# Broadcasting the decay rows in 2 KB pieces into the decay tiles, and alternating two PSUM banks, in a hybrid DeltaNet encoder layer

## The chip, the cores and the metric

The kernel runs on one core of one Trainium2 chip. The metric is device time in microseconds (us) for one execution, lower is better. Three executions were timed: 1382.4, 1386.79 and 1385.83 us, with a median of 1385.83 us.

## The reference, cut to what matters

One encoder layer over 512 positions of 1024 channels, batch 1, all in float32: a half-step SwiGLU FFN (width 2816), a token mixer, a second half-step FFN, a final RMSNorm. The mixer is where the change lies. One projection of the normed input gives, among others, q, k and v of 8 heads (128 channels each), which go through a short convolution of width 5 and SiLU. Each head then runs a gated delta rule over chunks, once left to right and once right to left:

```
qkv = silu(dwconv(dn_qkv, conv_dn));  q = l2norm(q) * DK**-0.5;  k = l2norm(k)
g = cumsum(-exp(a_log) * softplus(al + dt_bias))          # per chunk, per head, per direction
decay = exp(where(incl, g[..., :, None] - g[..., None, :], -inf))
a_mat = where(strict, (k*beta) @ k.T * decay, 0) + eye    # inverted by a triangular solve
attn  = (q @ k.T) * decay
state = state * exp(g_last) + (k * exp(g_last - g)).T @ v_new
```

So each head needs its cumulative decay g twice: as a column (one value per position, on partitions) and as a row broadcast over all 128 partitions, from which `decay` is made. It needs the products k·k and q·k within each chunk, the squares of k and q summed over channels, and k and v with positions on partitions.

## The kernel before, in words

Channels lie on partitions, 512 positions along the free dimension. Every weight product is done as three float32r matmuls (high part by high part, low by high, high by low; lines 186 to 188) over 128x128 weight tiles. `weight` loads 512 KB of raw weights into one of three `raw` buffers on SP's queue (L169), and ScalarE (ACT) and VectorE (DVE) split it into `hi` (L174) and `lo` (L176) in halves of 4 tiles, three buffers each. One raw load so feeds two hi/lo pairs, each pair 12 matmuls. These products fill TensorE (PE) through the whole program: first FFN, the mixer's 60 projections of 24 matmuls, the second FFN.

In the mixer the products are the filler between eight heads' DeltaNet work. `build(hd)` is a generator of ten steps: three short convolutions (each on one projection), SiLU of q, k and v and the decay broadcast, transposes of k, v and q to positions-on-partitions (`tok`), small per-head scales (`st`), the two decay tiles `ef` and `eb`, and twice (`c2`) a pair of chunks of key products. The table `EMIT` says in which sequence steps of `build` (b0 to b7), the triangular inversion (`invert`, for heads 0 to 2, 3 to 5, 6 and 7), `place`/`merge`, `scan` and the filler projections are recorded. The framework's scheduler then sets each engine's order from recorded order and priorities; weight loads and splits have a priority raised by 600. Within an engine, order is fixed: an instruction that waits holds all behind it, SP's queue of transfers too.

The decays: the cumulative decays `G` (128 positions by direction, chunk, head) are transposed on PE (L420), copied (L422) and written to DRAM as `grow` (L424). For each head, L469 reads its 8 rows of 128 values back into `Gb` (128 partitions by 8 by 128, 512 KB), every partition getting all 8 rows. `Gb` has one buffer, so a head's load waits for the last read of the head before. DVE reads it for `wj` and `el` in `st` (L514, L516) and for the subtraction into `ef` and `eb` (L528). ACT takes the exponentials of `st` (L517, L518), and Abs and Exp of `ef`, `eb` (L531 to L533).

The banks: PSUM has eight; three are `acc` for the products, two `ch` for the scan, and `o`, `kq`, `tp` one each. All transposes of `tok` go through `tp`: k, then v, then q. k's and q's transposes are also squared straight from the bank (L484), four ACT instructions each, so the bank stays taken until the last square:

```
                    if dst is not None:
                        act.copy(dst[:].rearrange("p c x -> p (c x)"), ps[:])
                    if sq is not None:
                        for c in range(NC):
                            act.activation(out=junk[:], in_=ps[:, c * P : c * P + P], func=ACT.Square,
                                           accum_out=ss[:, sq, c : c + 1])
```

Both pairs of chunks of key products (L547, L548) use the one bank `o`. It is read by `nl` (L552) and `at` (L556) on DVE, so the second pair's matmuls wait for the first pair's `at`. `kq` is used in the mixer by nothing else than a row-norm broadcast at its edges.

Of the kernel before, what the change touches and what calls it, by code (L numbers as in the profile page):

```python
# [7 lines left out]
F32 = mybir.dt.float32  # L8
F32R = mybir.dt.float32r
I32 = mybir.dt.int32  # L10
ACT = mybir.ActivationFunctionType
# [5 lines left out]
P = 128  # L17
# [5 lines left out]
NC = T // P  # L23
H = 8
# [29 lines left out]
def tile_layer(  # L54
# [23 lines left out]
    nc = tc.nc  # L78
    pe, act, dve, pool = nc.tensor, nc.scalar, nc.vector, nc.gpsimd

    def open_pool(stack, name, bufs=1, **kw):
        if "space" not in kw:
            kw["reuse_waits"] = "tile"
        return stack.enter_context(tc.tile_pool(name=name, bufs=bufs, **kw))
# [8 lines left out]
    psx = open_pool(ctx, "psx", bufs=1, space=PSUM)  # L93
    psum_ch = open_pool(ctx, "psum_ch", bufs=CH, space=PSUM)

    def bank(tag="acc", pool_=None):
        return (pool_ or psum).tile([P, 512], F32, tag=tag, name=tag, **({"bufs": TP} if tag == "tp" else {}))
# [14 lines left out]
    h = open_pool(first, "big", side="right").tile([P, KT, T], F32, tag="big", name="h")  # L112
# [12 lines left out]
    for k in range(KT):  # L125
# [3 lines left out]
        sq = sp0.tile([P, T], F32, tag="sq0", bufs=4, name="sq0")  # L129
# [6 lines left out]
    for i in range(2):  # L136
        ps = bank("o", psx) if i else bank("ch", psum_ch)
# [181 lines left out]
    def mixer(st, u, h, post):  # L319
# [3 lines left out]
        scr = open_pool(st, "scr", bufs=2, space=DRAM)  # L323
# [20 lines left out]
        wk = open_pool(dn, "wk", bufs=2)  # L344
        one = open_pool(dn, "one", bufs=1)
        with ExitStack() as dd:
            beta = dnc.tile([P, NC, 16], F32, name="beta")
            G = dnc.tile([P, 2, NC, H], F32, name="G")
# [15 lines left out]
            ps = bank("ch", psum_ch)  # L364
# [16 lines left out]
            ps = bank("tp", psx)  # L381
# [4 lines left out]
            x = dt.tile([P, NC, 16], F32, tag="spx", name="spx")  # L386
# [21 lines left out]
            for d in range(2):  # L408
                dve.scalar_tensor_tensor(
                    out=g[:, d], in0=x[:, :, d * H : d * H + H], scalar=-1.0,  # L410
                    in1=nea[:, d * H : d * H + H].unsqueeze(1).to_broadcast([P, NC, H]),
                    op0=ALU.mult, op1=ALU.mult)
            ps = bank("tp", psx)
# [5 lines left out]
            ps = bank("tp", psx)  # L419
            pe.transpose(ps[0:64, 0:P], G[:].rearrange("p d c h -> p (d c h)"), ident[:])  # L420
            gt = dt.tile([64, P], F32, tag="gt", name="gt")
            act.copy(gt[:], ps[0:64, 0:P])  # L422
            grow = scr.tile([2 * NC, H, P], F32, tag="grow", name="grow")
            nc.sync.dma_start(grow[:].rearrange("a h p -> (a h) p"), gt[:])  # L424
            early_half(T // 2, T)

        with dn:
# [20 lines left out]
            def short_conv(i):  # L448

                ps = project(12 + i)  # L450
                acc = cp.tile([P, T], F32, tag="cacc", name="cacc")
                taps(acc, ps, cvd_sb[:, i], 5)
                return acc

            def build(hd, s):
                cq = short_conv(hd)
                yield
                ck = short_conv(8 + hd)
                yield
                cv = short_conv(16 + hd)  # L460
                yield
# [3 lines left out]
                act.activation(out=kT[:], in_=ck[:], func=ACT.Silu)  # L465
                vT = cv
                act.activation(out=vT[:], in_=cv[:], func=ACT.Silu)
                Gb = wk.tile([P, 8, P], F32, tag="Gb", bufs=1, name="Gb")
                nc.sync.dma_start(Gb[:], grow[:, hd, :].unsqueeze(0).to_broadcast([P, 8, P]))  # L469

                yield

                ss = slot.tile([P, 2, NC], F32, tag="ss", name="ss")
                junk = one.tile([P, P], F32, tag="junk", name="junk")

                def tok(src, dst, sq):
                    ps = bank("tp", psx)
                    for c in range(NC):
                        pe.transpose(ps[:, c * P : c * P + P], src[:, c * P : c * P + P], ident[:])
                    if dst is not None:  # L480
                        act.copy(dst[:].rearrange("p c x -> p (c x)"), ps[:])
                    if sq is not None:
                        for c in range(NC):
                            act.activation(out=junk[:], in_=ps[:, c * P : c * P + P], func=ACT.Square,  # L484
                                           accum_out=ss[:, sq, c : c + 1])

                kt = s["kt"] = slot.tile([P, NC, P], F32, tag="kt", name="kt")
                tok(kT, kt, 0)
                vt = s["vt"] = slot.tile([P, NC, P], F32, tag="vt", name="vt")
                tok(vT, vt, None)  # L490
                tok(qT, None, 1)
                yield
                st_ = s["st"] = slot.tile([P, 8, 8], F32, tag="st", name="st")
# [8 lines left out]
                ns, sb, nr, wj, el = (st_[:, 2], st_[:, 3, 0:NC], st_[:, 4], st_[:, 5], st_[:, 6])  # L502
# [8 lines left out]
                dve.tensor_mul(brk, beta[:, :, hd], rk)  # L511
                for d in range(2):
                    last = (P - 1, 0)[d]
                    dve.tensor_sub(wj[:, d * NC : d * NC + NC], Gb[:, d * NC : d * NC + NC, last],  # L514
                                   G[:, d, :, hd])
                    dve.tensor_copy(el[:, d * NC : d * NC + NC], Gb[:, d * NC : d * NC + NC, last])  # L516
                act.activation(out=wj, in_=wj, func=ACT.Exp)  # L517
                act.activation(out=el, in_=el, func=ACT.Exp)  # L518

# [1 line left out]

                yield

                ef = wk.tile([P, NC, P], F32, tag="E", bufs=2, name="ef")
                eb = wk.tile([P, NC, P], F32, tag="E", bufs=2, name="eb")
                for d, m, op in ((0, ef, ALU.add), (1, eb, ALU.min)):
                    for c in range(NC):
                        dve.tensor_scalar(out=m[:, c, :], in0=Gb[:, d * NC + c, :],  # L528
                                          scalar1=G[:, d, c, hd : hd + 1], scalar2=0.0, op0=ALU.subtract,
                                          op1=op)  # L530
                act.activation(out=ef[:], in_=ef[:], func=ACT.Abs)  # L531
# [7 lines left out]
                nl = s["nl"] = slot.tile([P, 2, NC, P], F32, tag="nl", bufs=NL, name="nl")  # L539
                at = s["at"] = slot.tile([P, 2, NC, P], F32, tag="at", name="at")  # L540
                for c2 in range(2):
                    ps = bank("o", psx)
                    pk = ps[:].rearrange("p (c z x) -> p c z x", c=2, z=2)
                    for i in range(2):
                        c = 2 * c2 + i
                        sl = slice(c * P, c * P + P)
                        pe.matmul(pk[:, i, 0, :], kT[:, sl], kT[:, sl], start=True, stop=True)  # L547
                        pe.matmul(pk[:, i, 1, :], kT[:, sl], qT[:, sl], start=True, stop=True)  # L548
                    for i in range(2):
                        c = 2 * c2 + i  # L550
                        for d, m in ((0, ef), (1, eb)):
                            dve.scalar_tensor_tensor(out=nl[:, d, c, :], in0=pk[:, i, 0, :],  # L552
                                                     scalar=ns[:, d * NC + c : d * NC + c + 1],
                                                     in1=m[:, c, :], op0=ALU.mult, op1=ALU.mult)
                    for d, m in ((0, ef), (1, eb)):
                        dve.tensor_tensor(out=at[:, d, 2 * c2 : 2 * c2 + 2, :], in0=pk[:, :, 1, :],  # L556
                                          in1=m[:, 2 * c2 : 2 * c2 + 2, :], op=ALU.mult)
                    v = at[:, 0, 2 * c2 : 2 * c2 + 2, :]
                    pool.affine_select(out=v, in_=v, pattern=[[0, 2], [1, P]], compare_op=ALU.is_ge,
                                       fill=0.0, base=0, channel_multiplier=-1)  # L560
                    yield
# [398 lines left out]
    with ExitStack() as st:  # L960
        u, h, ssum = mixer(st, u2, h, ctx)
# [81 lines left out]
```

## Time and profile before

| what | value |
|---|---|
| median of three executions | 1385.83 us |
| the profiled execution: its own time, its span | 1384.16 us, 1382.1 us |
| PE busy / weight loads busy | 1339.7 us (97%) / 1112.8 us (81%) |
| DVE busy / ACT busy / POOL busy | 804.8 (58%) / 566.4 (41%) / 64.1 us (5%) |
| granted TensorE clock, mean over the span | 0.992 |
| DMA: moved, rate | 193.46 MB, mean 140 GB/s |
| mixer, from its first products to its merge | about 387 to 915 us of the span |

The page's first part gives each engine's busy time over the span. A busy PE of 97% says that PE is the engine to watch, and little of where the rest went: matmuls overlap in the records, so the start times in a timeline tell the pace. A window view gives the same figures for any stretch, with the granted clock and the DMA engines' busy share. The chain of waits runs back from the last instruction and names at each step what released it.

### The profile page before, as it was taken

The page shows a single profiled execution, that of the slowest core. Times are in us where ns is not written, and L with a number is a line of the kernel's source. Part 1 is how long each engine was busy: PE and PEld are TensorE (multiplying, and loading weights), DVE is VectorE, ACT ScalarE, POOL GpSimd, SP SyncE. Part 2 cuts the span into 40 slices and gives each one's busy share as a digit, 9 for nine tenths or more (in the row PEclk, how much of TensorE's full clock was granted, in tenths as well). Part 3 has the DMA queues.
Part 4 walks back from the last instruction along what each step waited for, and adds up shares of the span by engine and source line. Part 5 has one row for each costly group of instructions (what it writes and reads, how often), then busy time and mean ns, then how long its engine had stood idle before and what let it go on. Part 6 is the DMA issues. An engine that isn't in the chain of part 4 may idle for free.

```text
span 1382.1 us, 19594 instructions
## 1 busy us (share of the span) xinstructions
PE 1339.7 (97%) x7417; PEld 1112.8 (81%) x7417; DVE 804.8 (58%) x1745; ACT 566.4 (41%) x1150; POOL 64.1 (5%) x103
## 2 busy tenths in 40 slices
PE   6999999999998899999999999999999999999997
PEld 4888888888887778778777787888798888888886
DVE  6865555555375778786864785647553444443333
ACT  3333333322256664467555334545433333332330
POOL 0000000000000100021112001000000000000000
PEclk9999999999999999999999999999999999999999
DMA  8656566555434443333541433557503334333332
GB/s 319 218 159 191 181 193 191 171 172 182 130 126 94 124 130 127 121 116 107 130 139 60 124 113 95 168 197 245 176 31 104 125 109 134 124 108 95 100 100 71
DMA packets 86591, 193.46 MB, mean 140 GB/s; under 512 B 24737, under 2 KB 35169, under 8 KB 86370
## 3 DMA queue, kind: packets, MB, share of 16 engines
q1 hardware_dynamic: 71008, 164.29, 38.6%
q10 hardware_dynamic: 15490, 27.94, 5.9%
q8 instruction: 58, 0.95, 0.3%
q14 instruction: 35, 0.29, 0.1%
HBM read 171.19 MB, written 21.00 MB: 139 GB/s over the span
## 4 chain that ended last, share of the span: by engine, by line
PE 80%; DMA 8%; DVE 5%; issue 3%; ACT 3%; POOL 1%; ACTq 0%; POOLq 0%; SPq 0%; DVEq 0%
PE acc L188 22%; PE acc L186 22%; PE acc L187 22%; DMA msb<-gtd 2%; DMA Gb<-grow 2%; PE acc L918 1%; DVE lo L176 1%; PE ch L674 1%; PE ch L918 1%; PE o L697 1%; PE ch L685 1%; DMA raw<-w_in 1%; DVE cacc L444 1%; PE tp L610 1%; ACT hi L174 1%
## 5 line engine op out<-in xcount | busy, mean ns | idle before, releaser
L186 PE MATMUL acc<-uh,hi 128*128 128x512 f32 (+1 forms) x1224 | 473.3, 387 | 2.0 <-DVE sps L397 0.9
L187 PE MATMUL acc<-uh,lo 128*128 128x512 f32 (+1 forms) x1224 | 473.8, 387 | 0.7 <-DVE lo L176 0.7
L188 PE MATMUL acc<-ul,hi 128*128 128x512 f32 (+1 forms) x1224 | 472.3, 387 | 0.0
L174 ACT CAST hi<-raw 128x512 fp32r<-128x512 f32 (+1 forms) x416 | 252.2, 612 | 535.1 <-PE acc L188 479.0
L176 DVE TENSOR_TENSOR lo<-raw,hi 128x512 fp32r<-128x512 f32 (+1 forms) x416 | 280.4, 681 | 293.1 <-ACT hi L174 291.7
L186 PEld LDWEIGHTS acc<-uh,hi 128*128 128x128 f32 x1224 | 231.2, 189 | 44.4 <-ACT cacc L439 1.1
L187 PEld LDWEIGHTS acc<-uh,lo 128*128 128x128 f32 x1224 | 231.2, 189 | 42.3 <-DVE lo L176 1.3
L188 PEld LDWEIGHTS acc<-ul,hi 128*128 128x128 f32 x1224 | 230.8, 189 | 41.2
L186 PE MATMUL acc<-gh,hi 128*128 128x512 f32 (+1 forms) x396 | 144.9, 366 | 0.0
L187 PE MATMUL acc<-gh,lo 128*128 128x512 f32 (+1 forms) x396 | 144.6, 365 | 0.0
L188 PE MATMUL acc<-gl,hi 128*128 128x512 f32 (+1 forms) x396 | 144.4, 365 | 0.0
L150 DVE SCALAR_TENSOR_TENSOR raw<-raw,cs 128x1024 f32<-128x1024 f32 x72 | 87.9, 1223 | 59.8 <-DMA raw<-w_ada 59.7
L187 PEld LDWEIGHTS acc<-gh,lo 128*128 128x128 f32 x396 | 74.4, 188 | 12.1
L186 PEld LDWEIGHTS acc<-gh,hi 128*128 128x128 f32 x396 | 74.4, 188 | 12.1
L188 PEld LDWEIGHTS acc<-gl,hi 128*128 128x128 f32 x396 | 74.4, 188 | 12.1
L444 DVE SCALAR_TENSOR_TENSOR cacc<-acc,cvd_sb,cacc 128x510 f32<-128x510 f32 (+1 forms) x96 | 71.1, 742 | 4.3 <-ACT cacc L439 3.8
L313 DVE TENSOR_TENSOR sa<-sa,acc 128x512 f32<-128x512 f32 x40 | 27.4, 685 | 34.9 <-PE acc L188 33.2
L228 POOL TENSOR_TENSOR rs<-ms,mhalf 128x2 f32<-128x2 f32 (+1 forms) x7 | 6.2, 887 | 840.1 <-DVE ms L225 840.1
L196 ACT CAST gh<-sa 128x512 fp32r<-128x512 f32 x44 | 27.4, 622 | 18.4 <-DVE sa L313 13.7
L197 DVE TENSOR_TENSOR gl<-sa,gh 128x512 fp32r<-128x512 f32 x44 | 30.3, 692 | 5.5 <-PE tp L918 2.1
L206 ACT ACTIVATE sq<-h 128x512 f32<-128x512 f32 (+1 forms) x25 | 14.1, 563 | 47.3 <-DVE h L255 46.9
L584 DVE TENSOR_TENSOR A<-A,tmp 96x30 f32<-96x30 f32 (+29 forms) x90 | 29.0, 322 | 1.5
(270 smaller groups left out, 1454.4 us busy)
## 6 DMA issues: line engine op xcount, KB each, us to landing
raw<-w_ada SPq DMA_DIRECT2D x72, 512.0 KB
raw<-w_in SPq DMA_DIRECT2D x60, 512.0 KB
raw<-w2u SPq DMA_DIRECT2D x44, 512.0 KB
raw<-w1u SPq DMA_DIRECT2D x36, 512.0 KB
raw<-w1d SPq DMA_DIRECT2D x16, 512.0 KB
raw<-w2d SPq DMA_DIRECT2D x16, 512.0 KB
wf<-w1f SPq DMA_DIRECT2D x8, 512.0 KB
Gb<-grow SPq DMA_DIRECT2D x8, 512.0 KB
```

What stands on the lines that cost most here:

```text
L150: dve.scalar_tensor_tensor(out=raw[:], in0=raw[:], scalar=1.0, in1=cs[:], op0=ALU.mult, op1=ALU.mult, accum_out=part[:, n : n + 1])
L174: act.copy(hi[:], raw[:, k : k + n, :])
L176: dve.tensor_sub(lo[:], raw[:, k : k + n, :], hi[:].bitcast(F32))
L186: pe.matmul(ps[:, t0:t1], wh, rh[:, k0 + k, t0:t1], start=a, stop=False)
L187: pe.matmul(ps[:, t0:t1], wl, rh[:, k0 + k, t0:t1], start=False, stop=False)
L188: pe.matmul(ps[:, t0:t1], wh, rl[:, k0 + k, t0:t1], start=False, stop=b)
L196: act.copy(hi, src)
L197: dve.tensor_sub(lo, src, hi.bitcast(F32))
L313: dve.tensor_mul(sa[:], sa[:], ps[1][:])
L444: dve.scalar_tensor_tensor(out=acc[:, lo:hi], in0=src[:, lo + o : hi + o], scalar=w[:, i : i + 1], in1=acc[:, lo:hi], op0=ALU.mult, op1=AL ...
L584: dve.tensor_tensor(out=A[:, j + 1 : 32, 0:j], in0=A[:, j + 1 : 32, 0:j], in1=tv, op=ALU.add)
L918: pe.matmul(early[m][:], terms[i][0][:, m, :], terms[i][1], start=k == 0 and i == 0, stop=k == KT - 1 and i == 2)
```

## The change

`grow` becomes one row of 512 values per head and direction. Each head's broadcast is two transfers of 256 KB, straight into the tiles that become `ef` and `eb`, each partition getting 2 KB in one piece; they are recorded one to two steps earlier (after k's convolution) and those tiles have four buffers in place of two, `Gb` being gone. The subtraction works in place. v's transposes and the second pair of key products use bank `kq`. k's squares read the SBUF copy `kt`.

```diff
-            grow = scr.tile([2 * NC, H, P], F32, tag="grow", name="grow")
-            nc.sync.dma_start(grow[:].rearrange("a h p -> (a h) p"), gt[:])
+            grow = scr.tile([H, 2, NC * P], F32, tag="grow", name="grow")
+            nc.sync.dma_start(grow[:].rearrange("h d (c p) -> (d c) h p", p=P), gt[:])
...
                 ck = short_conv(8 + hd)
+
+                E = [wk.tile([P, NC, P], F32, tag="E", bufs=4, name=x) for x in ("ef", "eb")]
+                for d in range(2):
+                    nc.sync.dma_start(E[d][:].rearrange("p a b -> p (a b)"),
+                                      grow[hd, d : d + 1, :].to_broadcast([P, NC * P]))
...
-                Gb = wk.tile([P, 8, P], F32, tag="Gb", bufs=1, name="Gb")
-                nc.sync.dma_start(Gb[:], grow[:, hd, :].unsqueeze(0).to_broadcast([P, 8, P]))
...
-                def tok(src, dst, sq):
-                    ps = bank("tp", psx)
+                def tok(src, dst, sq, tag="tp"):
+                    ps = bank(tag, psx)
...
-                            act.activation(out=junk[:], in_=ps[:, c * P : c * P + P], func=ACT.Square,
-                                           accum_out=ss[:, sq, c : c + 1])
+                            act.activation(out=junk[:], in_=ps[:, c * P : c * P + P] if dst is None else dst[:, c, :],
+                                           func=ACT.Square, accum_out=ss[:, sq, c : c + 1])
...
-                tok(vT, vt, None)
+                tok(vT, vt, None, "kq")
...
-                    dve.tensor_sub(wj[:, d * NC : d * NC + NC], Gb[:, d * NC : d * NC + NC, last],
-                                   G[:, d, :, hd])
-                    dve.tensor_copy(el[:, d * NC : d * NC + NC], Gb[:, d * NC : d * NC + NC, last])
+                    dve.tensor_sub(wj[:, d * NC : d * NC + NC], E[d][:, :, last], G[:, d, :, hd])
+                    dve.tensor_copy(el[:, d * NC : d * NC + NC], E[d][:, :, last])
...
-                ef = wk.tile([P, NC, P], F32, tag="E", bufs=2, name="ef")
-                eb = wk.tile([P, NC, P], F32, tag="E", bufs=2, name="eb")
+                ef, eb = E
...
-                        dve.tensor_scalar(out=m[:, c, :], in0=Gb[:, d * NC + c, :],
+                        dve.tensor_scalar(out=m[:, c, :], in0=m[:, c, :],
...
-                    ps = bank("o", psx)
+                    ps = bank(("o", "kq")[c2], psx)
```

The scheduler gives a new order on every engine. Line numbers of the changed kernel differ by up to five (L469 becomes L462, L479 L481, L481 L483, L484 L486, L514 L516, L516 L517, L517 L518); L528 to L560 keep theirs. Three places follow.

**SP's queue of transfers, from the write of `grow` on** (L469 and L462 the broadcasts, L169 raw weights, L568 and L574 transfers of the inversion). Before, 9 rows:

```order
L424 DMA grow<-gt 64x128
L469 DMA Gb<-grow 128x8x128
L169 DMA raw<-w_in 128x1024
L469 DMA Gb<-grow 128x8x128
L169 DMA raw<-w_in 128x1024 x3
L568 DMA dl<-nl 128x1024
L574 DMA A<-dl 8x32x32
L169 DMA raw<-w_in 128x1024
L469 DMA Gb<-grow 128x8x128
```

Now:

```order
L424 DMA grow<-gt 8x8x128
L462 DMA ef<-grow 128x512
L462 DMA eb<-grow 128x512
L462 DMA ef<-grow 128x512
L462 DMA eb<-grow 128x512
L169 DMA raw<-w_in 128x1024 x3
L568 DMA dl<-nl 128x1024
L462 DMA ef<-grow 128x512
L169 DMA raw<-w_in 128x1024
L462 DMA eb<-grow 128x512
```

The broadcasts of heads 0 and 1 go out together right behind `grow`, and head 2's right behind head 0's `dl`, one raw load between its two halves.

**ACT, head 0's copies, squares and exponentials.** Before, 12 rows:

```order
L481 COPY kt<-tp 128x512
L484 ACTIVATE junk,ss<-tp 128x128
L517 ACT_TABLE_LOAD
L517 ACTIVATE st<-st 128x8
L484 ACTIVATE junk,ss<-tp 128x128
L518 ACTIVATE st<-st 128x8
L531 ACTIVATE ef<-ef 128x512
L174 CAST hi<-raw 128x512
L484 ACTIVATE junk,ss<-tp 128x128
L532 ACTIVATE ef<-ef 128x512
L484 ACTIVATE junk,ss<-tp 128x128
L533 ACTIVATE eb<-eb 128x512
```

Now:

```order
L483 COPY vt<-kq 128x512
L174 CAST hi<-raw 128x512
L483 COPY kt<-tp 128x512
L518 ACT_TABLE_LOAD
L518 ACTIVATE st<-st 128x8
L486 ACTIVATE junk,ss<-kt 128x128
L519 ACTIVATE st<-st 128x8
L531 ACTIVATE ef<-ef 128x512
L486 ACTIVATE junk,ss<-kt 128x128
L532 ACTIVATE ef<-ef 128x512
L486 ACTIVATE junk,ss<-kt 128x128
L533 ACTIVATE eb<-eb 128x512
```

The exponential of `st`, which needs the broadcast, still stands ahead of k's squares, but those squares no longer hold bank `tp`: the copy ahead of it does that alone. v's transposes now stand on PE ahead of the transposes that make `grow` (L420), in bank `kq`.

**DVE, where head 2's first read of the broadcast meets head 1's key products** (`nl` and `at` free the bank of the products). Before, 12 rows:

```order
L514 TENSOR_TENSOR st<-Gb,G 128x4
L516 COPY st<-Gb 128x4
L444 SCALAR_TENSOR_TENSOR cacc<-acc,cvd_sb,cacc 128x511
L514 TENSOR_TENSOR st<-Gb,G 128x4
L552 SCALAR_TENSOR_TENSOR nl<-o,st,ef 128x128
L444 SCALAR_TENSOR_TENSOR cacc<-acc,cvd_sb,cacc 128x510
L176 TENSOR_TENSOR lo<-raw,hi 128x512
L552 SCALAR_TENSOR_TENSOR nl<-o,st,eb 128x128
L552 SCALAR_TENSOR_TENSOR nl<-o,st,ef 128x128
L552 SCALAR_TENSOR_TENSOR nl<-o,st,eb 128x128
L556 TENSOR_TENSOR at<-o,ef 128x256
L556 TENSOR_TENSOR at<-o,eb 128x256
```

Now, 12 rows that begin with that read:

```order
L516 TENSOR_TENSOR st<-ef,G 128x4
L444 SCALAR_TENSOR_TENSOR cacc<-acc,cvd_sb,cacc 128x511
L176 TENSOR_TENSOR lo<-raw,hi 128x512
L444 SCALAR_TENSOR_TENSOR cacc<-acc,cvd_sb,cacc 128x511
L444 SCALAR_TENSOR_TENSOR cacc<-acc,cvd_sb,cacc 128x510 x2
L176 TENSOR_TENSOR lo<-raw,hi 128x512
L444 SCALAR_TENSOR_TENSOR cacc<-acc,cvd_sb,cacc 128x511
L552 SCALAR_TENSOR_TENSOR nl<-o,st,ef 128x128
L444 SCALAR_TENSOR_TENSOR cacc<-acc,cvd_sb,cacc 128x511
L552 SCALAR_TENSOR_TENSOR nl<-o,st,eb 128x128
L176 TENSOR_TENSOR lo<-raw,hi 128x512
L444 SCALAR_TENSOR_TENSOR cacc<-acc,cvd_sb,cacc 128x510
```

One read of head 2's broadcast still stands ahead of head 1's `nl` and `at`; its transfer stands much earlier in SP's queue, and the reads of its other half (L517, L516 of `eb`) now follow head 1's last `at`.

## Rows read from the trace of the kernel before

**Rows 1.** Windows: stretch, length, engines' busy (x instructions), granted clock, DMA share, GB/s.

```profile
430.00:510.00 80.00, 68.91 (x316) 56.12 (x315) 54.38 (x160) 50.80 (x120) 7.81 (x12) 0.91 0.45 115
...
442.00:448.00 6.00, 6.00 (x18) 4.80 (x18) 4.35 (x6) 4.25 (x7) 0.64 (x1) 0.55 0.43 89
...
448.00:470.00 22.00, 21.91 (x109) 18.14 (x108) 19.19 (x64) 17.05 (x46) 3.47 (x5) 1.00 0.43 135
```

**Rows 2.** Timeline of PE, first stall: start, us, instruction, [idle before <-releaser].

```profile
437.24 0.39 PE L186 MATMUL acc<-uh,hi 128*128 128x512 f32 x1
441.78 1.12 PE L479 MATMUL tp<-ident,cacc 128*128 128x128 f32 x4 [4.15 <-ACT junk L484]
...
447.66 0.40 PE L187 MATMUL acc<-uh,lo 128*128 128x512 f32 x1
...
448.56 0.39 PE L186 MATMUL acc<-uh,hi 128*128 128x512 f32 x1
448.79 0.40 PE L187 MATMUL acc<-uh,lo 128*128 128x512 f32 x1
```

**Rows 3.** Timeline of PE, one group of key products at full pace.

```profile
455.73 0.39 PE L547 MATMUL o<-kT 128*128 128x128 f32 x2
...
456.62 0.60 PE L479 MATMUL tp<-ident,qT 128*128 128x128 f32 x4
```

**Rows 4.** Timeline of PE, second and third stall.

```profile
474.55 0.39 PE L186 MATMUL acc<-uh,hi 128*128 128x512 f32 x1
478.36 0.77 PE L547 MATMUL o<-kT 128*128 128x128 f32 x2 [3.43 <-DVE at L556]
...
481.77 0.40 PE L188 MATMUL acc<-ul,hi 128*128 128x512 f32 x1
...
502.73 0.39 PE L188 MATMUL acc<-ul,hi 128*128 128x512 f32 x1
506.07 0.76 PE L547 MATMUL o<-kT 128*128 128x128 f32 x2 [2.96 <-DVE at L556]
...
509.06 0.40 PE L186 MATMUL acc<-uh,hi 128*128 128x512 f32 x1
```

**Rows 5.** The chain of waits: start, us, what; the broadcasts on it.

```profile
428.29 10.03 DMA Gb<-grow
...
464.64 9.63 DMA Gb<-grow
...
489.27 8.80 DMA Gb<-grow
```

**Rows 6.** Timelines of ACT and DVE: what the three broadcasts held up.

```profile
438.69 0.21 ACT L517 ACTIVATE st<-st 128x8 f32<-128x8 f32 x1 [4.10 <-DVE st L514]
...
474.29 0.17 DVE L514 TENSOR_TENSOR st<-Gb,G 128x4 f32<-128x4 f32 x1 [3.91 <-DMA Gb<-grow]
...
498.10 0.17 DVE L514 TENSOR_TENSOR st<-Gb,G 128x4 f32<-128x4 f32 x1 [3.62 <-DMA Gb<-grow]
```

**Rows 7.** A window during the first broadcast; ACT's queue in page part 3.

```profile
433.00:436.00 3.00, 3.00 (x15) 2.45 (x14) 0.00 (x0) 1.57 (x4) 0.00 (x0) 1.00 1.03 81
...
q10 hardware_dynamic: 15490, 27.94, 5.9%
```

**Rows 8.** Groups of convolution taps, `lo` splits, squares: count, busy us, mean ns, idle.

```profile
L176 DVE TENSOR_TENSOR lo<-raw,hi 128x512 fp32r<-128x512 f32 (+1 forms) x416 | 280.4, 681 | 293.1 <-ACT hi L174 291.7
...
L444 DVE SCALAR_TENSOR_TENSOR cacc<-acc,cvd_sb,cacc 128x510 f32<-128x510 f32 (+1 forms) x96 | 71.1, 742 | 4.3 <-ACT cacc L439 3.8
...
L484 ACT ACTIVATE junk<-tp 128x128 f32<-128x128 f32 x64 | 17.9, 280 | 5.4 <-PE tp L479 3.3 <-PE acc L187 1.0
...
L713 ACT ACTIVATE junk<-on 128x128 f32<-128x128 f32 x32 | 9.9, 308 | 6.8 <-DVE on L705 3.4 <-DVE rr L714 1.8 <-DVE A L584 1.1
```

**Rows 9.** Timelines of SP and ACT: a raw load held up, and its first cast.

```profile
616.63 1.20 SPq L169 DMA_DIRECT2D raw<-w_in  x2
...
632.29 0.62 ACT L174 CAST hi<-raw 128x512 fp32r<-128x512 f32 x1
```

## The prediction

> **What bounds the kernel now.** The busy times of the table above say that PE is busy for 97% of the span, so no other engine can set the end except by letting PE wait. The next question is where PE does not run at its pace, and the windows answer it: the stretch from 430 to 510 us has 68.91 us of PE in 80, at a mean granted clock of 0.91, where the mixer begins its heads [rows 1]. The reader should see that 11 us are missing there, and that what ran was partly at the lower clock. The timeline of PE through the mixer then shows three stops of over 1.5 us, all in this stretch. A product matmul at full pace starts 0.23 us after the last (448.56 to 448.79) [rows 2].
>
> First place: PE stands from 437.24, waiting 4.15 us for ACT's squares (L484) to leave bank `tp`; only at 447.66 is the pace back [rows 2]. After the stall the granted clock of 442 to 448 is 0.55, near the lower of the two levels (1.2 of 2.4 GHz) [rows 1]: PE had done nothing before. Between 437.24 and 447.66 lie 13 product matmuls and one group of four transposes. At pace these take 13 x 0.23 plus 0.44 (from 447.66 to 448.56 there are two products and one such group: 0.90 - 0.46), so 3.4 us. They took 10.4. **Loss: 7.0 us**, over half of it the wait, the rest the clock.
>
> Second and third: the second pair of key products waits for bank `o`, that is for DVE's `at`, 3.43 and 2.96 us [rows 4]. From 474.55 to 481.77 there are five product matmuls and a group of key products (0.89 us at pace [rows 3]), worth 5 x 0.23 + 0.89 = 2.0 us; they took 7.2: **loss 5.2 us**. From 502.73 to 509.06, four and a group, 1.8 us; they took 6.3: **loss 4.5 us** [rows 4].
>
> The three together are 16.7 us. What stands behind each is told by the chain of waits: the broadcast into `Gb` [rows 5]. It takes 10.03, 9.63 and 8.80 us to land, the second and third start only when DVE has read `Gb` for the head before, and what waits is: ACT, 4.10 us, for the scales (its squares of k stand behind them in order), and DVE, 3.91 and 3.62 us, with `nl` and `at` behind [rows 6].
>
> **The change, part by part.**
>
> *The broadcast in 2 KB pieces.* Bytes stay at 512 KB per head. While a broadcast ran, the 16 DMA engines were at 1.03 of their capacity and moved 81 GB/s [rows 7]: 243 KB cost 3.1 us of all sixteen, so a head's 524 KB some 6.7. ACT's queue, whose transfers here are nearly all 2 KB rows, put 27.94 MB through 5.9% of 1382.1 us [rows 7]: 2.9 us per MB, 1.5 us for a head. If the difference comes off the landing, 10.0 becomes about 4.9 us. The bounds: from below the 1.5 us of moving alone, from above no gain, 10.0. I take 5, since the saturated engines are the row nearest to the cause. The Trainium skill ("DMA: Bandwidth & Descriptors", Specifications) gives 512 B as the smallest transfer at line rate, and `Gb`'s pieces are 512 B, so by that rule the new pieces gain nothing and a head still takes 10 us. By that rule the engines should not be full at 81 GB/s, as the row has them.
>
> *Earlier, and four buffers.* Heads 0 and 1 get all four halves right behind `grow`, and head 2's wait no longer for head 1's subtraction but for head 0's `at`. In DVE's new order eight convolution taps and three `lo` splits stand, beside shorter work, between that `at` and the first read of head 2's half: 8 x 0.74 + 3 x 0.68 = 8.0 us [rows 8]. A landing of 5 us leaves 3 of slack. The waits of DVE on the second and third broadcast go; behind a 10 us landing some 2 us each would stay.
>
> *The banks.* k's squares no longer hold `tp`, and v's transposes stand in `kq`, before `grow` is even written. PE's next use of `tp` needs only the copy of k, which ACT makes ahead of the exponential. So the first stall loses both its causes, and a late broadcast no longer reaches PE at that point. The second pair of key products goes to `kq` and doesn't wait for `at` of the first pair. Each of the second and third stall loses both causes too.
>
> *What it adds.* (a) Eight more DMA issues on SP, under half a microsecond each; SP waits most of the time. (b) 32 squares read SBUF: 308 ns in place of 280 [rows 8], 0.9 us of ACT over the whole mixer, hidden behind PE's products; on the path it would be those 0.9. (c) New waits for banks: `tp` waits for k's copy where q's transposes follow closely; `kq` is shared by v's transposes and key products, and in four heads only a few product matmuls stand between the one and the other. From below nothing; from above a copy behind a cast, both as long as the cast's 0.62 us [rows 9], in each of seven heads: 8.7 us. I take 2, half a microsecond in four heads. (d) The subtraction in place and the strided reads keep their shapes: nothing. (e) Density: with the stalls gone, the 54.4 us of DVE and 50.8 of ACT in this stretch [rows 1] must fit into 63, 86% and 81%. The stretch from 448 to 470 ran with DVE at 87% and ACT at 78%, and PE lost 0.1 us in 22 [rows 1]. I take 1 us, between 0 and 6.
>
> **Sum.** 16.7 - 2 - 1 = 13.7 us off. The profiled execution took 1384.2 us (span 1382.1 and 2.1 around it), so 1370.5; the median shown is 1.7 above it, which gives **1372 us**. Bounds of this case: all recovered and nothing added, 1369; with the upper ends of (c) and (e), 14.7 us given back and 2 won, 1384; the likely part of it is 1369 to 1377.
>
> **The rivals.**
>
> *The pieces land no sooner.* Both halves of head 0 are in at 438, as before, and each later head takes 9 to 10 us. For: a broadcast reads one row 128 times, which none of the 2 KB loads here does. Against: [rows 7]. (The Trainium skill's 512 B rule of "DMA: Bandwidth & Descriptors", Specifications, would have it so.) ACT's 4.10 us of waiting [rows 6] stay; `tp` no longer hangs on them, only k's SiLU of head 1, whose transposes PE reaches 48 products (11 us) later, so half of it, 2 us, may reach PE. DVE's 2 us each at heads 2 and 3 reach it by half, as only the next head's key products wait. Time: 1372 + 4 = 1376.
>
> *DVE or ACT becomes the bound.* The stalls were also when DVE and ACT got ahead. If the denser stretch makes PE wait for `lo` or `hi`, the waits come back in small pieces, and as the clock falls after longer ones, they double. With 10 to 16 us returned: 1382 to 1386. For: 86% as a mean over 63 us, in strict order. Against: the stretch of 448 to 470 [rows 1].
>
> *Slower: SP's queue.* A half of `ef` waits for `at` two heads back, in SP's order, and raw loads stand behind it. In the new order the middle heads have one place where two raw loads are followed by two `dl`, a head's broadcast, and some twelve small transfers of the inversion before the next raw load; before there was a raw load in between. The old queue had the nearest such hold, and it was harmless: the raw load issued at 616.63 was first read 15.7 us later, at 632.29 [rows 9]; with the slowest landing of the rows, 10.03 [rows 5], 5 to spare. The mechanism decides once the new hold is over 5 us longer. Then each further us stops PE and the clock falls after it; to end slower by 0.3% it must eat the 13.7 and 4 more, two such places of about 9 us each: 1390.
>
> *It does not do what it says.* If the scheduler's order put the reads of `ef` so early that DVE waits as long as before, times would be the old ones, 1384 to 1386; the order shown speaks against it for the first three heads.
>
> **How the numbers follow.** A time within 0.3%, 4.2 us, is about what a measurement of this kernel can't tell from no change. Chances: my forecast 0.62, late landing 0.13, density 0.12, SP's queue 0.08, no effect 0.05. Faster: the first two, and a quarter of density, 0.78. Slower: SP's queue, and a little of density where the order is unlucky, 0.10. The rest, 0.12, is same. The range from 1367 to 1381.5 takes in the forecast with its bounds and late landing, and the better end of density; 1367 allows for two or three us of small waits elsewhere in the mixer that a new order may drop.
>
> **What would show it.** Right: from 430 to about 495 no idle of PE over 1 us and a granted clock of 1.00; no wait of DVE or ACT for `ef` or `eb`; those transfers landing within about 5 us; DVE's share near 86%. Idle of PE behind `tp`, `o` and `kq` under 3 us in all from 430 to 915. The stretches of the two FFNs keep their length. Wrong: PE idle before products on `lo` or `hi` in that stretch (density); a long wait for a broadcast on DVE (late landing); casts that wait for raw loads near 600 to 650 (SP's queue).

## The result and the profile after

The changed kernel took 1373.25 us (median of four executions, 1372.13 to 1378.47) beside 1385.6 us for the kernel before (median of four). The ratio is 0.993, with a 95% interval of 0.9906 to 0.9954: 12 us faster. Its profiled execution took 1372.99 us, that of the kernel before 1384.16 (spans 1371.2 and 1382.1), at a mean granted clock of 0.996 (0.992 before). Two executions far off the rest, one of the kernel before at 4695 us and one of the late-place version (e6 below) at 2242 us, are left out of every median below.

The windows of the changed kernel, with the columns of [rows 1]; the last one lies inside the first broadcasts, as [rows 7] does for the kernel before:

```profile
430.00:510.00 80.00, 79.92 (x396) 66.38 (x395) 65.90 (x185) 62.28 (x137) 10.07 (x14) 1.00 0.50 150
442.00:448.00 6.00, 6.00 (x31) 4.79 (x30) 5.41 (x22) 4.08 (x12) 1.80 (x2) 1.00 0.29 87
...
600.00:650.00 50.00, 46.83 (x352) 38.48 (x350) 29.02 (x99) 33.33 (x83) 7.39 (x11) 0.97 0.35 114
...
431.00:433.00 2.00, 2.00 (x16) 1.79 (x15) 0.51 (x2) 1.22 (x3) 0.00 (x0) 1.00 0.95 345
```

From 430 to 510 us PE is busy for 79.92 of 80 us where it was 68.91, at full clock, and 442 to 448, once at 0.55, has 31 PE instructions where it had 18. DVE (82%) and ACT (78%) carry the denser stretch without making PE wait. During the first broadcasts the DMA engines move 345 GB/s in place of 81.

The timelines of SP and DVE, head 0's two halves:

```profile
428.97 0.33 SPq L462 DMA_DIRECT2D ef<-grow  x1
429.34 0.43 SPq L462 DMA_DIRECT2D eb<-grow  x1
...
432.50 0.16 DVE L516 TENSOR_TENSOR st<-ef,G 128x4 f32<-128x4 f32 x1 [1.58 <-DMA ef<-grow]
...
433.25 0.16 DVE L516 TENSOR_TENSOR st<-eb,G 128x4 f32<-128x4 f32 x1
```

The first half is read 3.5 us after its issue and the second at most 3.9, with head 1's halves sharing the engines; the old load took 10.03 [rows 5]. DVE's 1.58 us is its only wait for a broadcast. The waits of [rows 6] and the stalls of [rows 2, 4] are gone.

What was won can be followed through the program by the start of each cast on L174 in ACT's timeline, n-th cast against n-th cast (416 in each kernel). The lead over the kernel before is -0.1 us where the mixer starts (387 us), 16.0 at 519, 8.1 at 593, 9.0 at 918 and 11.6 at the end. **Sixteen microseconds are won, and seven of them are given back inside the mixer.** Casts stand in another order here, so single values inside the mixer wander by some us; those at its two ends and the last do not depend on it.

The 2.6 us that return behind the mixer can't be put down to the change. There PE waits for the sums of a row norm, 2.5 us in the kernel before, after which the granted clock fell, and 1.5 us here, after which it did not. Another execution of the changed kernel (e9 below) has the same wait of 1.5 us and a lower clock, so this part differs from one execution to the next. The windows of the kernel before, the changed kernel and e9:

```profile
980.00:1010.00 30.00, 27.30 (x178) 25.15 (x176) 19.62 (x39) 13.08 (x26) 0.69 (x1) 0.94 0.43 144
...
980.00:1010.00 30.00, 28.02 (x232) 27.47 (x231) 20.82 (x48) 11.94 (x26) 1.59 (x2) 1.00 0.22 72
...
980.00:1010.00 30.00, 28.48 (x213) 27.96 (x212) 19.98 (x46) 11.75 (x26) 1.56 (x2) 0.89 0.21 70
```

The five largest waits of PE from 510 to 920 us show where it now stops (in us: total, times, longest):

```profile
PE tp L724 <- DVE on L719: 3.4, 4, 1.6
PE ch L685 <- DVE yw L682: 1.8, 1, 1.8
PE tp L610 <- DVE t L604: 0.8, 1, 0.8
PE o L547 <- DVE at L556: 0.8, 1, 0.8
PE ch L674 <- DVE r L670: 0.6, 1, 0.6
```

A stop is counted here where the instruction behind a product starts more than 0.25 us later than the pace of 0.23 us. These stops add up to 11.7 us in 15 places, where the kernel before had 3.9 in 8. (Stops behind other work are not counted; with them it is 12.0 against 6.0.) The largest is this one, PE's timeline first, then ACT's:

```profile
633.64 0.40 PE L186 MATMUL acc<-uh,hi 128*128 128x512 f32 x1
635.79 0.79 PE L685 MATMUL ch<-yw,kt 128*128 128x128 f32 x2 [1.76 <-DVE yw L682]
636.38 0.63 PE L668 MATMUL ch<-S,kT 128*128 128x128 f32 x2
...
628.20 0.45 ACTq L732 DMA_DIRECT2D ybd<-z  x1
...
634.98 0.37 ACT L679 ACTIVATE y<-ch,st 128x128 f32<-128x128 f32 x1 [2.94 <-DMA ybd<-z]
```

PE waits for `yw`, which DVE makes from `y`; ACT makes `y` late, because the load of `z` ahead of it in its order waits 2.94 us for the store of the head before (`z` has one buffer). The matmuls behind the stop are slower (0.63 us), and the window from 600 to 650 is at 0.97.

### The profile page after: what moved, and what is told of

The parts are those of the page before. It is cut to its first block, busy times and chain, and to the rows that moved or that the text cites. A ratio compares the mean times of both kernels' runs of the same rounds, so it can differ in the third digit from the quotient of the medians.

```text
span 1371.2 us, 19599 instructions
## 1 busy us (share of the span) xinstructions
PE 1336.6 (97%) x7417; PEld 1109.4 (81%) x7417; DVE 801.8 (58%) x1745; ACT 566.3 (41%) x1150; POOL 65.3 (5%) x103
## 5 line engine op out<-in xcount | busy, mean ns | idle before, releaser
L174 ACT CAST hi<-raw 128x512 fp32r<-128x512 f32 (+1 forms) x416 | 252.1, 612 | 533.8 <-PE acc L188 486.7
L188 PEld LDWEIGHTS acc<-gl,hi 128*128 128x128 f32 x396 | 74.4, 188 | 11.8
L206 ACT ACTIVATE sq<-h 128x512 f32<-128x512 f32 (+1 forms) x25 | 14.1, 563 | 47.6 <-DVE h L255 47.2
L582 DVE TENSOR_TENSOR tmp<-A 96x30 f32<-96x30 f32 (+29 forms) x90 | 29.0, 322 | 1.2
```

The lines of the kernel that those rows point to most:

```text
L174: act.copy(hi[:], raw[:, k : k + n, :])
L188: pe.matmul(ps[:, t0:t1], wh, rl[:, k0 + k, t0:t1], start=False, stop=b)
L206: act.activation(out=sq[:], in_=hk, func=ACT.Square)
L582: dve.tensor_tensor(out=tv, in0=A[:, j + 1 : 32, j : j + 1].to_broadcast([nb, n, j]), in1=A[:, j : j + 1, 0:j].to_broadcast([nb, n, j]), o ...
```

## The experiments

All ratios are to the kernel before on the same chip in the same job (medians 1384.13, 1383.15 and 1383.09 us).

**The two parts apart.** The broadcast part without the bank part, and the bank part on the kernel before:

```diff
# e1_broadcast_only, against the changed kernel
-act.activation(out=junk[:], in_=ps[...] if dst is None else dst[:, c, :],
+act.activation(out=junk[:], in_=ps[...],
-tok(vT, vt, None, "kq")
+tok(vT, vt, None)
-ps = bank(("o", "kq")[c2], psx)
+ps = bank("o", psx)
# e2_banks_only: the opposite three lines, against the kernel before
```

> The changed kernel without its bank part: all transposes in tp, squares from the bank, both pairs of key products in o; the 2 KB broadcasts, early and in four buffers, stay. Theory A (the broadcast's lateness is the cause behind all three stalls, the banks only pass it on): the three stalls of PE near 441, 478 and 506 us shrink to under 1.5 us each, no wait of ACT over 1 us for the scales and none of DVE for the tiles; 10 to 13 us off the kernel before (1373 to 1376). Theory B (the banks carry the gain, the broadcast only moves DVE's wait): stalls of 2 to 4 us stay on tp and o, 0 to 4 us off (1381 to 1386).

> The kernel before with the bank part alone: v's transposes and the second pair of key products in kq, k's squares from SBUF; Gb stays as it was (512 B pieces, one buffer, late). Theory A: ACT still waits some 4 us for the first broadcast and DVE 3 to 4 us each for the second and third, and lo and hi come late behind them; PE loses 6 to 12 us in this stretch, elsewhere than at tp and o; 4 to 10 us off (1376 to 1382). Theory B: PE no longer stops in this stretch although DVE waits; 11 to 14 us off (1372 to 1375).

The broadcast alone: 1372.95 us, ratio 0.9929 (0.9904 to 0.9954), as fast as the whole change. The banks alone: 1379.78 us, 0.9973 (0.9957 to 0.9989). Their windows, the broadcast first:

```profile
430.00:510.00 80.00, 79.86 (x396) 66.37 (x395) 66.26 (x184) 63.67 (x138) 10.10 (x14) 1.00 0.48 149
```

```profile
430.00:510.00 80.00, 75.52 (x369) 61.90 (x368) 60.05 (x174) 52.71 (x126) 7.79 (x12) 1.00 0.46 132
```

With the banks alone the stops are shorter but there (the profiled execution, 1386.96 us, was the slowest of its twelve). In one of the two largest PE's transposes wait for k's SiLU:

```profile
449.08 0.66 PE L479 MATMUL tp<-ident,kT 128*128 128x128 f32 x4 [1.61 <-ACT kT L465]
```

So the banks shield PE from a late broadcast in part; with a quick one nothing is left to shield.

**The changed kernel with 512 B pieces.** `grow` has its old layout; place, buffers and banks are the new ones, and PE, DVE, ACT and POOL have the order of the changed kernel:

```diff
# e3_small_pieces, against the changed kernel
-grow = scr.tile([H, 2, NC * P], ...)
+grow = scr.tile([2 * NC, H, P], ...)
-nc.sync.dma_start(E[d]..., grow[hd, d : d + 1, :].to_broadcast([P, NC * P]))
+nc.sync.dma_start(E[d][:], grow[d * NC : d * NC + NC, hd, :].unsqueeze(0).to_broadcast([P, NC, P]))
```

> The changed kernel with grow in its old layout, so each half of a head's broadcast comes in four pieces of 512 B per partition in place of one of 2 KB; order on every engine is that of the changed kernel. Theory A (the 512 B pieces fill the engines): a head's two halves land some 9 to 10 us after issue in place of 4, DVE waits for ef and eb near 435 to 438; 2 to 6 us slower than the changed kernel (1375 to 1379). Theory C (early issue and four buffers hide the landing, piece size is worth nothing): within 1.5 us of the changed kernel. Theory D (piece size carries all): 10 us or more slower (1383 and up).

1381.74 us, 0.9981 (0.9968 to 0.9995). The timeline of DVE:

```profile
434.60 0.17 DVE L516 TENSOR_TENSOR st<-ef,G 128x4 f32<-128x4 f32 x1 [3.17 <-DMA ef<-grow]
...
438.00 0.17 DVE L516 TENSOR_TENSOR st<-eb,G 128x4 f32<-128x4 f32 x1 [2.56 <-DMA eb<-grow]
```

Issued at 428.94 and 429.37, the halves are read after 5.7 and 8.6 us in place of 3.5 and 3.9. At heads 1 and later DVE waits for no broadcast. Issuing earlier, into more buffers and with the second bank, is worth 2.4 us without larger pieces. That lies between the 1379 of Theory A and the 1383 of Theory D: the pieces carry most of it.

**Two buffers for the decay tiles** in place of four (`tag="E", bufs=2`):

> The changed kernel with two buffers of the decay tiles in place of four, still issued after k's convolution: a head's broadcast waits for the head before to have made its at. Theory A (what counts is that DVE never waits for a landing): DVE waits 3 to 5 us per head at heads 1 to 3 and lo comes late behind it; PE stops again for 4 to 12 us in all between 440 and 510; 4 to 10 us slower than the changed kernel (1377 to 1383). Rival (the piece size and the banks alone do it, prefetch adds nothing): within 2 us of the changed kernel.

1375.56 us, 0.9937 (0.9919 to 0.9955), and 79.91 us of PE in the window from 430 to 510. DVE waits twice for a broadcast, 2.6 us in all, and PE does not stop for it. I had expected a loss of 4 to 10 us; it can't be told from the changed kernel.

**The pieces alone.** The kernel before with another layout of `grow` and nothing else. PE, DVE, ACT and POOL keep their order word for word:

```diff
# e5_pieces_alone (e10_pieces_here is the same kernel), against the kernel before
-grow = scr.tile([2 * NC, H, P], ...)
-nc.sync.dma_start(grow[:].rearrange("a h p -> (a h) p"), gt[:])
+grow = scr.tile([H, 2 * NC, P], ...)
+nc.sync.dma_start(grow[:].rearrange("h a p -> a h p"), gt[:])
-nc.sync.dma_start(Gb[:], grow[:, hd, :].unsqueeze(0).to_broadcast([P, 8, P]))
+nc.sync.dma_start(Gb[:]..., grow[hd : hd + 1].rearrange("h a x -> h (a x)").to_broadcast([P, 8 * P]))
```

> The kernel before with one thing changed: grow is stored as one row of 1024 values per head, so that a head's broadcast reads each partition's 4 KB in one piece. Gb, its one buffer, its place in SP's queue and the banks stay; the instructions of PE, DVE, ACT and POOL stand in the same order as before. Theory P (piece size alone sets when the data is there): the broadcast lands some 4 us after its issue in place of 8.8 to 10.0, DVE's and ACT's waits of 3.6 to 4.1 us for it fall under 1 us, the three stops of PE shrink to under 1 us each; 1373 to 1376 us, that is 8 to 11 us under the kernel before. Theory E (early issue and pieces are both needed, since a head's broadcast here still waits for the last read of the head before): the first stop goes, and of the second and third 1 to 2 us each are left, with the clock falling after them; 1377 to 1381. If the piece size does nothing by itself: 1383 to 1386.

**1369.05 us, 0.99 (0.9878 to 0.9922): better than the changed kernel**, and better than I expected of it. Its chain of waits has the second and third broadcast (start, us), which took 9.63 and 8.80 us before [rows 5]:

```profile
456.98 6.69 DMA Gb<-grow
...
477.20 5.60 DMA Gb<-grow
```

At 6.69 and 5.60 us they land later than the 4 us that I expected, beside other transfers. Even so no wait of DVE for `Gb` is over 1.0 us in this run (before 5.66 at head 0, then 3.91 and 3.62 [rows 6]), and no stop of PE from 430 to 510 has over 0.5 us of waiting.

**The late place.** The changed kernel with the two broadcasts recorded where the old one stood:

```diff
# e6_late_place, against the changed kernel
                 ck = short_conv(8 + hd)
-                E = [wk.tile(...) ...]
-                for d in range(2):
-                    nc.sync.dma_start(E[d]..., grow[hd, d : d + 1, :]...)
...
                 act.activation(out=vT[:], in_=cv[:], func=ACT.Silu)
+                E = [wk.tile(...) ...]
+                for d in range(2):
+                    nc.sync.dma_start(E[d]..., grow[hd, d : d + 1, :]...)
```

> The changed kernel with the two broadcasts of a head recorded where the kernel before has its one (after the SiLU of v); 2 KB pieces, four buffers and the banks stay. The scheduler gives a new order, so 1 or 2 us of this may be order. Theory P (piece size alone): no wait of DVE for a broadcast over 1.5 us, PE's windows from 430 to 510 as in the changed kernel, 1371 to 1376 us. Theory E (the early place is needed as well): DVE waits 2 us or more for the first half of heads 0 or 1, PE stops of 1 to 2 us return in 430 to 510; 1377 to 1381.

1375.3 us, 0.9939 (0.9917 to 0.996). DVE waits 0.65 us for `ef`, PE has 79.88 of 80 us in 430 to 510. The early place is not needed, and its absence doesn't bring the 1369 either.

**Two buffers for z**, against the stop at 635, with two for E to make room; once with the banks, once without:

```diff
# e7_two_z; e8_two_z_no_banks takes out the bank part as e1 does
-SL, NL, RAW, ZB, CP, FLB = 5, 5, 3, 1, 6, 2
+SL, NL, RAW, ZB, CP, FLB = 5, 5, 3, 2, 6, 2
-E = [wk.tile([P, NC, P], F32, tag="E", bufs=4, ...
+E = [wk.tile([P, NC, P], F32, tag="E", bufs=2, ...
```

> The changed kernel with two buffers for E (as in the run before of that kind) and two for z, so that the load of z on ACT's queue need not wait for the store of the z of the head before. Theory Z (this hold is where some of the gain is given back in the scan): the wait of 2.9 us on ACT for the store of z near 635 us is gone, PE's stop on ch behind it (1.8 us, and the lower clock after it) too; 1369 to 1373 us, 2 to 4 under the run with two E buffers alone. Rival (the give-back is spread over the scan's chains on DVE, and when this stop goes the next chain stops PE by as much): 1373 to 1376, no difference from the run with two E buffers alone that can be told.

> As the run with two z buffers, but without the bank part of the change (k, v and q through tp, both pairs of key products through o, squares from the bank): the smallest version, as the banks alone were worth little. Theory Z: 1368 to 1372 us, at most the run of the broadcast alone (1373) less 2 to 4. Rival (spread): 1372 to 1376. If the banks matter once the other holds are gone: 2 or more us above the run with two z buffers and the banks.

1375.98 us (0.9946, 0.9929 to 0.9963) and 1374.6 us (0.9934, 0.9915 to 0.9953). My theory of the z hold falls: the hold is gone from ACT, the time isn't. The window from 600 to 650 of e7 has as little of PE as in the changed kernel, and its timeline other stops, on casts and splits:

```profile
600.00:650.00 50.00, 46.46 (x355) 38.25 (x354) 31.93 (x105) 30.99 (x76) 7.62 (x11) 0.97 0.42 119
```

```profile
619.89 0.51 PE L186 MATMUL acc<-uh,hi 128*128 128x512 f32 x1 [1.13 <-ACT hi L174]
622.47 0.53 PE L187 MATMUL acc<-uh,lo 128*128 128x512 f32 x1 [2.07 <-DVE lo L176]
```

**Side by side.** The changed kernel and the pieces alone on one chip, with two further versions of the pieces:

```diff
# e11_pieces_and_banks: e5 with the three lines of the bank part
# e12_two_transfers: the kernel before with the changed kernel's grow, and two 2 KB transfers into Gb
+[nc.sync.dma_start(Gb[:, d * NC : d * NC + NC, :]..., grow[hd, d : d + 1, :].to_broadcast([P, NC * P])) for d in range(2)]
```

> The changed kernel itself, unaltered, on the same chip as the next run, because a difference of 4 us between two jobs is near what such a comparison can tell. Theory O (the changed kernel's order of work, made by the scheduler for the earlier broadcasts, costs 3 to 5 us in the scan whatever the broadcast does): 1372 to 1376 us here, and 3 to 5 us above the run of the pieces alone beside it. Rival (the difference between the jobs was the chip): within 1.5 us of the pieces alone.

> The kernel before with nothing but 4 KB pieces of the broadcast, unaltered from the earlier run, on the same chip as the changed kernel. Theory O: 1368 to 1371 us, again 3 to 5 us under the changed kernel, with PE's busy time in the window from 600 to 650 us near 49 of 50 where the changed kernel has 47. Rival: 1371 to 1375, no difference from the changed kernel.

> The kernel before with 4 KB pieces and the bank part of the change; Gb, its one buffer and the old place of the broadcast stay. The order of work is that of the run with the banks alone. If the banks still buy something once the broadcast is quick (they remove PE's remaining waits of 1.6 us in all for DVE's at): 1 to 2 us under the pieces alone, 1366 to 1368. If the banks only bring another order: 1369 to 1374, equal or above.

> The kernel before with the changed kernel's layout of grow and its two transfers of 2 KB pieces per head, but into Gb, at the old place, with one buffer and no bank part. The scheduler moves some of the work round them, so this is a third order. If 2 KB pieces are as good as 4 KB and the order does not matter: 1368 to 1371. Theory O (each new order of the scan costs or gains a few us by itself): anywhere from 1368 to 1377, with no wait of DVE for Gb over 2.5 us and no stop of PE over 1 us from 430 to 510, so that what differs lies after 510.

| run | median, us | ratio (95%) | order on PE | stops 510 to 920, us (places) | lead of casts at 387, 519, 918, end, us |
|---|---|---|---|---|---|
| e9, changed kernel | 1374.22 | 0.9933 (0.9918 to 0.9948) | new | 11.8 (15) | -0.7, 16.0, 9.1, 10.3 |
| e10, pieces alone | 1367.18 | 0.989 (0.9873 to 0.9907) | as before | 3.6 (7) | -1.0, 16.4, 16.8, 18.1 |
| e11, pieces and banks | 1373.11 | 0.993 (0.9913 to 0.9946) | new | 8.3 (11) | 0.1, 17.5, 13.4, 15.7 |
| e12, two transfers | 1367.63 | 0.9888 (0.9873 to 0.9903) | as before | 3.2 (6) | -0.3, 17.5, 18.2, 18.1 |

Stops and leads are worked out as above, from the one profiled execution of each; e11's was the shortest of its six, 1369.13 us, and e10's the shortest of its four. e12's order on PE is that of the kernel before but for a buffer's number; on ACT and DVE some instructions of the first heads move. The intervals of e9 and e10 don't overlap: the changed kernel is **7 us slower than large pieces alone**, and between 519 and 918 it gives back the same 7 us (16.0 to 9.1), where e10 and e12 give back nothing. PE's waits from 510 to 920 in e10, and the window from 600 to 650:

```profile
PE tp L724 <- DVE on L719: 3.0, 3, 1.3
PE o L547 <- DVE at L556: 0.6, 2, 0.4
```

```profile
600.00:650.00 50.00, 48.97 (x377) 40.73 (x375) 33.94 (x106) 38.42 (x92) 9.56 (x13) 1.00 0.43 138
```

Two piece sizes by three orders, each as its median less that of the kernel before in the same job; the four engines' orders are equal within a row, but e2 and e3 ran on another chip than e9, e10 and e11:

| order of PE, DVE, ACT, POOL | 512 B pieces | 2 or 4 KB pieces | pieces are worth |
|---|---|---|---|
| of the kernel before | 0 (before) | -15.9 us (e10) | 15.9 us |
| of the banks alone | -4.4 us (e2) | -10.0 us (e11) | 5.6 us |
| of the changed kernel | -2.4 us (e3) | -8.9 us (e9) | 6.5 us |

With small pieces the changed kernel's order and buffers win 2.4 us; with large pieces they cost 7.0. Every other version with large pieces and a new order on PE (e1, e4, e6, e7, e8, e11) is 7.2 to 11.2 us under the kernel before of its job, whichever part of the change it has, and the changed kernel itself 12.4 and 8.9 in its two comparisons; the two versions that keep the old order, in three measurements, 14.1 to 15.9. What the change wins, its layout wins. What else it does costs 6 to 7 us side by side (e9 and e11 against e10 and e12), and 2 to 9 over all jobs. That it does so by giving the scheduler another order is argued, not shown by itself: the bank part alone brings the loss (e11), and so do the early broadcasts without it (e8, with two z buffers, 5.5 us above e5 in the same job); what these versions share is a new order. Which feature of that order does it is open: one stop was taken away (e7), and others took its place.

## Why the prediction was right, and where it was not

**The stalls and their cause: right.** Three stops, 16.7 us, all caused by the late broadcast. Speeding the broadcast up, with nothing else changed, gave a lead of 17.4 us (e10, -1.0 to 16.4) and 17.8 (e12) by 519 us, and 15.9 in the median. Counting the products and pricing them at pace, clock loss included, was the right measure of the stall; the wait alone (4.15 + 3.43 + 2.96 = 10.5 us) would have been too little.

**The landing: right in size, not in its reason.** The estimate was 4.9 us for a head, bounds 1.5 to 10.0. A whole head is read 4.1 us after its issue in e10, in one transfer (e5's later ones took 6.69 and 5.60):

```profile
429.26 0.33 SPq L469 DMA_DIRECT2D Gb<-grow  x1
...
433.38 0.16 DVE L514 TENSOR_TENSOR st<-Gb,G 128x4 f32<-128x4 f32 x1
```

The step took the saved engine time off the landing, since the engines stood full in one window [rows 7]. Two other windows of the kernel before, inside the first and the third broadcast of [rows 5], have them a third busy at nearly the same rate:

```profile
429.50:432.00 2.50, 2.49 (x14) 1.81 (x13) 1.13 (x3) 2.49 (x5) 0.00 (x0) 1.00 0.34 75
...
491.00:496.00 5.00, 5.00 (x27) 4.26 (x26) 2.91 (x12) 2.48 (x6) 1.62 (x2) 1.00 0.33 75
```

At 75 to 81 GB/s, with a share of 0.33 or of 1.03, it was not full engines that held the small pieces back, and the 6.7 us of moving, worked out from one window, are not their price. That 4.9 came out so near is partly luck. What holds them back is open: 75 GB/s is 146 pieces of 512 B in a microsecond and 345 GB/s 168 of 2 KB, so the pieces pass at about the same rate (an estimate from these rows), but 268 GB/s is only 65 of 4 KB. The runs also change where the pieces lie in DRAM (512 B pieces lie apart, large ones are one row), so the size itself and the place were not tried apart.

The price of moving 2 KB pieces, taken from ACT's queue as 2.9 us per MB, stands beside 345 GB/s at a share of 0.95 after, which is 2.75 us per MB at full engines. The Trainium skill's 512 B rule ("DMA: Bandwidth & Descriptors", Specifications) would have had the pieces land no sooner. Here it doesn't hold: with the order on PE, DVE, ACT and POOL unchanged, going from 512 B to 4 KB took the first broadcast from 10.03 to at most 4.1 us, and 15.9 us off the kernel.

**"Earlier, and four buffers": not needed.** The step expected DVE's waits on the second and third broadcast to go, and behind a 10 us landing some 2 us each to stay. With small pieces (e3) these two waits go as well, so the early issue does hide a slow landing from head 1 on. With quick pieces there is nothing to hide: one buffer, the old place and a quick landing leave DVE no wait over 1.0 us (e5, e12), and PE none over 0.5. Two buffers do as well as four (e4), and the late place as the early one (e6).

**"Each of the second and third stall loses both causes too": one sufficed.** The bank part is worth 4.4 us by itself in that job and nothing on top of quick pieces; e11 is 6 us above e10.

**The terms (c), 2 us for waits at banks, and (e), 1 us for density: mis-sized and in the wrong place.** Density cost nothing: 79.92 of 80 us. PE's waits behind `tp`, `o` and `kq` come to 6.1 us from 430 to 915, where the prediction's sign was under 3. Of these, 4.2 us behind `tp` in the rows after were for DVE's `on` and `t`, in scan and inversion (3.3 in the kernel before), and none for k's copy. What these terms stood for, the price of all that is not the broadcast, is 7 us by the leads between 519 and 918 and 7 by the medians of e9 and e10, where they had 3; the bounds (0 to 8.7 and 0 to 6) took it in. The prediction compared the orders in three places near the broadcasts and gave the scan, 100 us later, no term of its own. That a forecast of 13.7 us met 12.4 is partly luck: beside e10 the same kernel won 8.9, and in the first profiled pair 2.6 us of the lead came behind the mixer.

**The rivals.** "The pieces land no sooner" was put at 1376; e3, which makes it so, took 1381.7. Its 4 us counted half of each wait, at heads 0, 2 and 3. In e3 DVE waited at head 0 alone; PE lost 3.0 us in 430 to 510 (77.00 of 80), and the rest came after 510, with 15.1 us of stops in 21 places (in a profiled execution of 1385.83 us, the slowest of its twelve). SP's queue as the slower side did not show: no cast waits for a raw load on the changed kernel's ACT from 500 to 915 us. Density did not show either. Of the other signs, one wait of DVE for `ef` was there (1.58 us, where none was forecast), and DVE's share was 82% in place of 86.

## What to carry to other kernels

When the chain shows a late load, repair the load first and leave everything else in its place: here three lines, the layout of a scratch tensor and its read, were worth 16 us, and the rest of the change cost 7 of them. Where a scheduler orders the engines, every added buffer, bank or moved line is also a new order, so compare orders through the whole stage, and time the edit in a version whose order is unchanged. A lead followed instruction by instruction through the program tells what was won from what was given back, which a median can't.

## What the hardware showed that was not expected

The same broadcasts move at 75 to 81 GB/s in 512 B pieces, at 345 in 2 KB pieces (share 0.95) and, beside other transfers, at 268 in 4 KB pieces (share 0.85, e10 from 431 to 433). 2 and 4 KB give the same time (e12, e10). The busy share is no steady measure of it: with 512 B pieces it was 1.03 [rows 7], 0.34 and 0.33 (rows above) and, at another place (e3, 433 to 436), 0.59 at 79 GB/s. With small pieces, in the same order, ACT's wait at 635 for the store of `z` was longer as well: 4.71 us in e3, 2.94 in the changed kernel. That the broadcasts in flight did this is likely, but was not tried.
